# Two-block model on one core: the order of router, gather and tail in the experts, and of the matmuls in a feed-forward loop

## The chip, the core and the metric

One core of one Trainium2 chip runs the whole program in one launch. The metric is the device time of an execution in microseconds, as the median of several runs. The engines are named as in the profile: PE is TensorE (matmuls), PEld its loads of stationary operands, DVE VectorE, ACT ScalarE, POOL GpSimd, SP the engine whose queue issues most of the large loads. Everything is computed in float32; the large products split an operand into a high and a low part and add the products of the parts.

## The reference, cut to what matters

One sequence of 256 tokens with 1024 features passes through two blocks. The first block holds the experts that the change is about; the second is two layers, each with a feed-forward half, a mixing part and a second feed-forward half.

```python
# block 1
h = x
u = rmsnorm(h, norm_mix_g) @ w_in
o_sb = sb_group(u[..., :SB_IN], sb_out_g)          # stick-breaking attention
o_rw = rwkv7_group(u[..., SB_IN:], ...)            # a delta-rule recurrence
h = h + concatenate([o_sb, o_rw]) @ w_out
xn = rmsnorm(h, norm_ffn_g).reshape(256, 1024)
y = hier_moe(xn, ...)
h = rmsnorm(h + y, final_norm_g)

def hier_moe(x, w_grp, b_grp, w_exp, b_exp, w_gate, w_up, w_down):
    # 4 groups of 8 experts: the best group, then the best 2 of its 8
    grp_prob = softmax(x @ w_grp + b_grp);  g_val, g_idx = top_k(grp_prob, 1)
    sel = the 8 columns of (x @ w_exp + b_exp) that belong to g_idx
    e_val, e_idx = top_k(softmax(sel), 2)
    weights = g_val * e_val / sum(e_val)
    combine = for each token the weight of each of the 32 experts (30 are zero)
    for e in range(32):                            # w_gate, w_up: 1024x256, w_down: 256x1024
        y += combine[:, e:e+1] * ((silu(x @ w_gate[e]) * (x @ w_up[e])) @ w_down[e])

# block 2, the part that the change touches, four times
swiglu(x, w_gate, w_up, w_down) = (silu(x @ w_gate) * (x @ w_up)) @ w_down   # 1024 -> 2816 -> 1024
```

## The kernel before, in words

The 256 tokens are two blocks j = 0, 1 of 128, and the 1024 features are two halves n = 0, 1 of 512. `x` holds the residual stream, tokens on partitions.

**End of the projection (L936 to L954).** The output projection adds eight 128-row pieces f of `w_out` into four accumulators `acs[j, n]`. The pieces f = 4 to 7 come last, as the list `us`. Block 0 is finished first; for each half, `router.add` adds the residual and takes the squares, and `router.factor(0)` makes the factor of the norm. Then the half (1, 0) of the projection runs, then block 0's transposes (`turn`) and their copy out of PSUM (`turned`), then half (1, 1), and then the 16 small matmuls `logits` of block 0, eight for each half, with 36 columns (4 groups and 32 experts).

**Router (L983 to L1012, and L1273 to L1306).** Inside `Moe.run`, block 1 goes through the same steps. `select(j)` is a list of 12 small VectorE steps that picks group and experts; `ranks(j)` gives each token its slot in its expert, from two small matmuls with a triangular matrix, and `place` turns that into a one-hot matrix `OH[j]`. Each expert has 32 slots. `weave` issues the steps of two lists in turn. The three `with_x` matmuls that stand in between seed the accumulators `py[j, n]` with `x`; the fourth stands in round 0.

**Rounds (L1311 to L1347).** There are eight rounds q of four experts. `up` multiplies the gathered rows of four experts with gate (hf = 0) and up (hf = 1) matrices, 32 matmuls for each expert and round and half, the four experts on four strips of 32 rows. `act` makes silu(gate) * up * weight, transposes it and copies it to `hT`. `down` multiplies with the down matrices, for the two output halves one after the other. `back` splits a half into a high and a low part (`yh`, `yl`) and adds it into `py[j, n]` by a matmul with the transposed one-hot matrix, which brings the rows back to their tokens. The rows of the next round are gathered in the same round: `gather` multiplies `OH[j]` with `x` for j = 0, 1 and both halves into one PSUM tile `mx`, `gathered` copies half 0 by ScalarE and half 1 by VectorE into `xr`, and `rows_T` transposes `xr` and writes the gained rows `XG`.

**Weights (L1026 to L1052).** There are 96 loads of 1 MB: in each round four gate, four up and four down matrices. They go through the SP queue into 22 ring places, taken in the order of `order`. `load_next` issues the next ones as soon as the code has finished with older ones; a load waits until the place that it overwrites has been read. The places lie where the pools of the projection lie, so that the first 22 loads wait for the projection's tiles. One of those tiles is `kk0` (L436), which shares its memory with place `mw8`, the sixth in the order. The down matrix of expert 31, the last, is loaded in two halves of 512 output columns.

**Tail (L1350 to L1395).** After the last round the result stands in `py`. `gained` multiplies it with the final gain, `square` and `square_x` take the eight sums of squares that the final norm and the next norm need, and `back(7, y, 1)` stands behind the first `gained`.

**Order.** What is issued between `K.ordered = True` and `K.ordered = False` on PE, DVE and ACT keeps the order of the code (`keep_in_program_order`). Everything else, the loads on SP and POOL too, is put in order by the framework's planner from its estimates. The framework also orders accesses to one tile from the code, and adds the waits between engines.

**Feed-forward loop (L1728 to L1746).** A step i makes 256 of the 2816 hidden columns of gate and up, for both blocks; there are ten steps in each of four loops. Its weights come in four units of two 128-row pieces (`wh`, `wl`: the high and low part). For each unit, eight wide matmuls (512 columns: `wh` with both parts of X) and then eight narrow ones (256 columns: `wl` with the high part) are issued, over the four combinations of b (128 columns of the hidden ones) and s (gate or up).

Of the kernel before, what the change touches and what calls it, by code (L numbers as in the profile page):

```python
# [9 lines left out]
F32 = mybir.dt.float32  # L10
# [7 lines left out]
P = 128  # L18
# [287 lines left out]
class Front:  # L306
# [112 lines left out]
    def run(self, ctx, x, router):  # L419
# [523 lines left out]
        for n in range(2):  # L943
            if n:
                for h in range(2):
                    router.turn(x, 0, h)
                for h in range(2):
                    router.turned(0, h, xT[h])
            for f, u in us:
                out_mm(u, f, 1, n, False, f == 7)  # L950
        for n in range(2):
            router.logits(0, n, xT[n])
        K.ordered = False
        router.rest = [acs[1, n] for n in range(2)]  # L954
# [6 lines left out]
class Moe:  # L961
# [52 lines left out]
    def run(self, ctx, x, B=None):  # L1014
# [103 lines left out]
        def gather(q, j):  # L1118

            if j == 0:  # L1120
                pg[0] = K.mx.tile([P, 2, 512], F32, name="mx")
            for n in range(2):
                K.mm(pg[0][:, n], OH[j][:, 4 * q:4 * q + 4].rearrange("p e c -> p (e c)"), x[:, j, n * 512:(n + 1) * 512],
                     j == 0, j == 1, share=True)

        def gathered():
            xr[0] = wk.tile([P, 2, 512], F32, name="xr")
            V, S, _ = K.engines()
            S.activation(xr[0][:, 0], pg[0][:, 0], AF.Copy)
            V.tensor_copy(xr[0][:, 1], pg[0][:, 1])  # L1130

        def rows_T():

            pt = K.mx.tile([P, KD, P], F32, name="mx")
            r = xr[0].rearrange("p n f -> p (n f)")
            V, S, T_ = K.engines()
# [63 lines left out]
        def all_tokens(nmax):  # L1200
            v = nc.values_load(nmax[0:1, 0:1], min_val=0, max_val=2 * T)
            with tc.If(v > CAP):
# [7 lines left out]
                with tc.For_i(0, NE, 1) as e:  # L1210
# [13 lines left out]
                    for j in range(2):  # L1224
                        hT = self.act(wk, a[j], ce[:, j], self.r[j])
# [13 lines left out]
        def down(q, hT):  # L1239
            ys = []  # L1240
            for n in range(2):
                y = K.mx.tile([P, 512], F32, name="mx")
                for k in range(2):
                    for i in range(4):
                        K.mm(y[32 * i:32 * i + 32], hT[:, k, 32 * i:32 * i + 32],
                             W["d", 4 * q + i, 0][:, k, n * 512:(n + 1) * 512], k == 0, k == 1, share=True)
                ys.append(y)
            return ys
# [12 lines left out]
        def back(q, ys, n):  # L1261
            if q == 7 and n:
                t = spare("yr", 12, F32R)
                yh, yl = t[:, 0:512], t[:, 512:1024]
            else:
                yh, yl = [wk.tile([P, 512], F32R, name=t) for t in ("yh", "yl")]
            K.engines()[1].activation(yh, ys[n], AF.Copy)
            K.engines()[0].tensor_sub(yl, ys[n], yh)
            for y in (yh, yl):
                for j in range(2):  # L1270
                    K.mm(py[j, n], OHT[0][:, q % 2, j * P:(j + 1) * P], y, False, q == 7 and y is yl)

        K.ordered = True  # L1273
        xT = [wk.tile([P, 4, P], F32, name="xTm", tag=t) for t in ("XG1", "yh")]
# [3 lines left out]
        for n in range(2):  # L1278
            self.add(x, 1, n, self.rest[n], self.rest[n])
        for n in range(2):  # L1280
            self.turn(x, 1, n)
            self.turned(1, n, xT[n])
        for n in range(2):
            self.logits(1, n, xT[n])
        f1 = self.factor(1)
        run(f1[:4])
        weave(f1[4:], s0[:6])
        for n in range(2):
            with_x(0, n)
        weave(s0[6:], s1[:6])  # L1290
        K.mm(pr[:, 0], lt, mask[:, 0])
        K.mm(pr[:, 1], K.ones, mask[:, 0], stop=False, share=True)
        with_x(1, 0)
        run(s1[6:8])
        weave(s1[8:10], ranks(0))
        run(s1[10:])
        K.mm(pr[:, 1], lt, mask[:, 1], start=False, share=True)
        gather(0, 0)
# [7 lines left out]
        def rows(q):  # L1306
            for j in range(2):
                gather(q, j)
# [1044 lines left out]
```

## Time and profile before

| | |
|---|---|
| median of 3 runs | 1621.58 us (1621.26 to 1625.19) |
| profiled execution | 1625.12 us |
| its span | 1623.4 us |
| mean granted clock of PE | 0.981 of full speed |
| PE, DVE, ACT, POOL busy | 95%, 64%, 51%, 3% |
| DMA | 331.29 MB, mean 204 GB/s |

The span is the time from the first to the last instruction in the trace of one profiled execution; times in the rows further down count from its start. A row names the engine, the line of the code, the operation, the output and input tiles, and in brackets the idle time before it and what ended it. L48 stands for everything that is issued in the pinned order, since the helper on that line issues it. The experts lie between about 223 us, where the projection ends, and 447 us, where the final norm's first multiply starts; the four feed-forward loops begin at 464.48, 862.36, 1048.62 and 1446.89 us in the chain of waits.

### The profile page before, as it was taken

The numbers are of one execution on the slowest core, as the hardware profiler recorded it, in microseconds if no ns is written. First come the engines' busy times: TensorE is split into PE (matmuls) and PEld (weight loads), VectorE is DVE, ScalarE is ACT, GpSimd is POOL, SyncE is SP. The second block draws the span as 40 slices with busy tenths as digits, with TensorE's granted clock in tenths as the row PEclk, the third lists the DMA queues.
The fourth block names the chain that finished last, engine by engine and source line by source line (L and its number), as shares of the span: only waits on it lengthen the run. The fifth ranks groups of instructions, "written<-read, shape, count | busy, mean of one in ns | idle before, by whom it ended". The sixth has DMA issues, their size and how long they took to land.

```text
span 1623.4 us, 25106 instructions
## 1 busy us (share of the span) xinstructions
PE 1549.9 (95%) x9734; PEld 1283.6 (79%) x9734; DVE 1036.6 (64%) x1916; ACT 828.3 (51%) x1408; POOL 43.5 (3%) x134
## 2 busy tenths in 40 slices
PE   7999998887799999999999999999999999999998
PEld 6989874343378888889878888888888989778887
DVE  7866551111377656868986665666648779876653
ACT  6633421111356544668645554456546687455643
POOL 4000000000100000000000000000000000000000
PEclk9999998999999999999999999999999999999999
DMA  6431599999956555553456665656566434556653
GB/s 209 136 102 66 202 369 388 421 420 420 374 182 194 182 194 176 181 163 104 156 182 195 185 196 183 202 182 185 176 203 203 157 118 151 173 157 188 197 178 111
DMA packets 195644, 331.29 MB, mean 204 GB/s; under 512 B 11972, under 2 KB 150674, under 8 KB 183362
## 3 DMA queue, kind: packets, MB, share of 16 engines
q1 hardware_dynamic: 186208, 315.19, 56.4%
q0 software_dynamic: 4528, 13.41, 2.5%
q8 instruction: 77, 1.26, 0.3%
q10 hardware_dynamic: 4786, 1.05, 0.3%
q14 instruction: 45, 0.37, 0.1%
HBM read 328.25 MB, written 1.38 MB: 203 GB/s over the span
## 4 chain that ended last, share of the span: by engine, by line
PE 70%; DMA 6%; DVE 4%; ACT 2%; issue 1%; SPq 0%; ACTq 0%; DVEq 0%
PE acc L246 39%; PE mx L246 19%; PE acc L48 7%; PE mx L48 4%; DMA mw<-in_exp_w_down 2%; DMA mw<-in_exp_w_up 1%; DMA mw<-in_exp_w_gate 1%; DVE wl L258 1%; DVE wl L48 1%; PE mx L1969 0%; DMA wr<-in_w_in 0%; ACT wh L277 0%; PE mx L1993 0%; DMA wr<-in_ffn_w_up 0%; DVE ul L258 0%
## 5 line engine op out<-in xcount | busy, mean ns | idle before, releaser
L258 DVE TENSOR_TENSOR wl<-wr,wh 128x1024 fp32r<-128x1024 f32 x358 | 436.7, 1224 | 269.8 <-ACT wh L277 267.3
L277 ACT ACTIVATE wh<-wr 128x1024 fp32r<-128x1024 f32 x358 | 377.9, 1058 | 363.3 <-PE acc L246 249.5
L246 PE MATMUL acc<-X,wh 128*128 128x256 f32 (+1 forms) x1664 | 357.1, 329 | 0.0
L246 PEld LDWEIGHTS acc<-X,wh 128*128 128x128 f32 x1664 | 277.2, 191 | 25.4 <-issue 4.2
L246 PE MATMUL acc<-X,wl 128*128 128x256 f32 x1152 | 237.2, 284 | 0.0
L246 PEld LDWEIGHTS acc<-X,wl 128*128 128x128 f32 x1152 | 186.3, 191 | 6.9
L246 PE MATMUL mx<-X,wh 128*128 128x512 f32 x640 | 161.9, 393 | 0.0
L246 PEld LDWEIGHTS mx<-X,wh 128*128 128x128 f32 x640 | 114.5, 189 | 19.9
L246 PE MATMUL acc<-wh,hh 128*128 128x512 f32 x288 | 112.1, 389 | 0.0
L246 PE MATMUL acc<-wl,hh 128*128 128x512 f32 x288 | 112.1, 389 | 0.0
L246 PE MATMUL acc<-wh,hl 128*128 128x512 f32 x288 | 112.0, 389 | 0.0
L246 PEld LDWEIGHTS mx<-X,wl 128*128 128x128 f32 x640 | 88.3, 190 | 7.0
L246 PE MATMUL mx<-X,wl 128*128 128x256 f32 x640 | 90.5, 282 | 0.0
L48 PE MATMUL mx<-mw,XG 128*32 128x256 f32 x1024 | 64.6, 396 | 9.3 <-DMA mw<-in_exp_w_up 5.9
L48 PEld LDWEIGHTS mx<-mw,XG 128*32 128x32 f32 x1024 | 34.2, 114 | 37.9 <-issue 9.2
L246 PEld LDWEIGHTS acc<-wh,hl 128*128 128x128 f32 x288 | 54.1, 188 | 11.3
L246 PEld LDWEIGHTS acc<-wh,hh 128*128 128x128 f32 x288 | 54.1, 188 | 11.2
L246 PEld LDWEIGHTS acc<-wl,hh 128*128 128x128 f32 x288 | 54.1, 188 | 11.0
L246 PE MATMUL acc<-wh,m 128*128 128x512 f32 x192 | 61.4, 394 | 0.0
L48 DVE COPY xr<-mx 128x512 f32<-128x512 f32 x8 | 5.5, 691 | 74.1 <-ACT xr L48 74.1
L246 PE MATMUL acc<-xh,wh 128*128 128x256 f32 x176 | 50.3, 286 | 0.0
L246 PE MATMUL acc<-xh,wl 128*128 128x256 f32 x176 | 49.9, 283 | 0.0
(641 smaller groups left out, 2537.4 us busy)
## 6 DMA issues: line engine op xcount, KB each, us to landing
wr<-in_w_in SPq DMA_DIRECT2D x44, 1024.0 KB, 5.4
wr<-in_ffn_w_gate SPq DMA_DIRECT2D x88, 512.0 KB, 4.0
wr<-in_ffn_w_up SPq DMA_DIRECT2D x88, 512.0 KB, 5.1
wr<-in_ffn_w_down SPq DMA_DIRECT2D x40, 1024.0 KB, 5.0
mw<-in_exp_w_gate SPq DMA_DIRECT2D x32, 1024.0 KB, 14.8
mw<-in_exp_w_up SPq DMA_DIRECT2D x32, 1024.0 KB, 16.7
mw<-in_exp_w_down SPq DMA_DIRECT2D x31, 1024.0 KB, 17.6
wr<-in_w_out SPq DMA_DIRECT2D x20, 1024.0 KB, 5.0
```

Source lines behind the costliest of these rows:

```text
L48: return lambda *a, **k: self.tc.keep_in_program_order(f(*a, **k))
L246: self.engines()[2].matmul(out, l, r, start=start, stop=stop, skip_group_check=share)
L258: i = self.K.engines()[0].tensor_sub(l, v, h)
L277: self.K.engines()[1].activation(h, v[:, q:q + c], AF.Copy)
```

## The change

Five things change their place in the order; no large product is added or taken away.

- Router: block 0's transposes and logits move ahead, between the pieces of the projection's halves (1, 0) and (1, 1), and so do the add, the transposes, the copy and the logits of block 1's half 0. The new tile `xT1` holds that half; it borrows the place `kk0`. In `Moe.run` only half 1 of block 1 is left, and `select(0)` and `ranks(0)` run around it.
- Gather: `gather(q, j, n)` does one half at a time, and the copy of a half follows the second matmul of that half. In each round `act` yields behind the multiply (a generator now): the matmuls with block 0's rows stand between the multiply and the transposes of the activation, those with block 1's rows and the copies behind `hT`. `rows_T` stands behind the down matmuls of the second output half. The three `with_x` move into round 0, ahead of its down matmuls.
- Down and back: the first output half's copies (`out_rows`) are issued ahead of the second half's down matmuls. In round 7 the second half leaves out the fourth expert, whose two matmuls come in the tail, behind the first half's `back`.
- Tail: `gained` of half 0 comes first for both blocks, then the squares of (0, 0), then the rest of round 7's second half in pinned order, then the other squares, with `square_x(1, 0)` last.
- Feed-forward loop: for each (b, s) the two wide matmuls and then the two narrow ones, in place of eight wide and eight narrow ones in a row.

```diff
@@ -940,18 +940,27 @@
         run(router.factor(0))
-        for n in range(2):
-            if n:
-                for h in range(2):
-                    router.turn(x, 0, h)
-                for h in range(2):
-                    router.turned(0, h, xT[h])
-            for f, u in us:
+        def last(n, fu):
+            for f, u in fu:
                 out_mm(u, f, 1, n, False, f == 7)
-        for n in range(2):
-            router.logits(0, n, xT[n])
+        last(0, us[:2])
+        for h in range(2):
+            router.turn(x, 0, h)
+        for h in range(2):
+            router.turned(0, h, xT[h])
+        last(0, us[2:])
+        for h in range(2):
+            router.logits(0, h, xT[h])
+        last(1, us[:2])
+        router.rest = acs[1, 1]
+        router.add(x, 1, 0, acs[1, 0], acs[1, 0])
+        router.turn(x, 1, 0)
+        xT1 = ft([4, P], "xT1", "kk0")
+        router.turned(1, 0, xT1)
+        last(1, us[2:])
+        router.logits(1, 0, xT1)
         K.ordered = False
-        router.rest = [acs[1, n] for n in range(2)]
 NRING = 22
@@ -1115,25 +1124,25 @@
         XG, pg, xr = [None, None], [None], [None]
-        def gather(q, j):
-            if j == 0:
+        def gather(q, j, n):
+            if j + n == 0:
                 pg[0] = K.mx.tile([P, 2, 512], F32, name="mx")
-            for n in range(2):
-                K.mm(pg[0][:, n], OH[j][:, 4 * q:4 * q + 4].rearrange("p e c -> p (e c)"), x[:, j, n * 512:(n + 1) * 512],
-                     j == 0, j == 1, share=True)
-        def gathered():
-            xr[0] = wk.tile([P, 2, 512], F32, name="xr")
-            V, S, _ = K.engines()
-            S.activation(xr[0][:, 0], pg[0][:, 0], AF.Copy)
-            V.tensor_copy(xr[0][:, 1], pg[0][:, 1])
+            K.mm(pg[0][:, n], OH[j][:, 4 * q:4 * q + 4].rearrange("p e c -> p (e c)"), x[:, j, n * 512:(n + 1) * 512],
+                 j == 0, j == 1, share=True)
+            if j:
+                V, S, _ = K.engines()
+                if n:
+                    V.tensor_copy(xr[0][:, n], pg[0][:, n])
+                else:
+                    xr[0] = wk.tile([P, 2, 512], F32, name="xr")
+                    S.activation(xr[0][:, n], pg[0][:, n], AF.Copy)
         def rows_T():
             pt = K.mx.tile([P, KD, P], F32, name="mx")
+            V, S, T_ = K.engines()
             r = xr[0].rearrange("p n f -> p (n f)")
-            V, S, T_ = K.engines()
             for k in range(KD):
...
@@ -1236,16 +1245,11 @@
                          W["gu", 4 * q + i, hf][:, k], k + hf == 0, k == KD - 1, share=True)
-        def down(q, hT):
-            ys = []
-            for n in range(2):
-                y = K.mx.tile([P, 512], F32, name="mx")
-                for k in range(2):
-                    for i in range(4):
-                        K.mm(y[32 * i:32 * i + 32], hT[:, k, 32 * i:32 * i + 32],
-                             W["d", 4 * q + i, 0][:, k, n * 512:(n + 1) * 512], k == 0, k == 1, share=True)
-                ys.append(y)
-            return ys
+        def down_mm(q, hT, y, n, experts):
+            for k in range(2):
+                for i in experts:
+                    K.mm(y[n][32 * i:32 * i + 32], hT[:, k, 32 * i:32 * i + 32],
+                         W["d", 4 * q + i, 0][:, k, n * 512:(n + 1) * 512], k == 0, k == 1, share=True)
         def spare(name, slot, dt=F32):
@@ -1258,55 +1262,51 @@
             K.mm(py[j, n], K.ident, x[:, j, n * 512:(n + 1) * 512], True, False)
-        def back(q, ys, n):
+        yp = {}
+        def out_rows(q, y, n):
             if q == 7 and n:
                 t = spare("yr", 12, F32R)
-                yh, yl = t[:, 0:512], t[:, 512:1024]
+                yp[n] = t[:, 0:512], t[:, 512:1024]
             else:
-                yh, yl = [wk.tile([P, 512], F32R, name=t) for t in ("yh", "yl")]
-            K.engines()[1].activation(yh, ys[n], AF.Copy)
-            K.engines()[0].tensor_sub(yl, ys[n], yh)
-            for y in (yh, yl):
-                for j in range(2):
-                    K.mm(py[j, n], OHT[0][:, q % 2, j * P:(j + 1) * P], y, False, q == 7 and y is yl)
+                yp[n] = [wk.tile([P, 512], F32R, name=t) for t in ("yh", "yl")]
+            V, S, _ = K.engines()
+            S.activation(yp[n][0], y[n], AF.Copy)
+            V.tensor_sub(yp[n][1], y[n], yp[n][0])
+        def back(q, n):
+            yh, yl = yp[n]
+            for j, y in [(0, yh), (0, yl), (1, yh), (1, yl)] if q == 7 else [(0, yh), (1, yh), (0, yl), (1, yl)]:
+                K.mm(py[j, n], OHT[0][:, q % 2, j * P:(j + 1) * P], y, False, q == 7 and y is yl)
         K.ordered = True
-        xT = [wk.tile([P, 4, P], F32, name="xTm", tag=t) for t in ("XG1", "yh")]
+        xT = wk.tile([P, 4, P], F32, name="xTm", tag="XG1")
         OH[0] = K.xp.tile([P, NE, CAP], F32, name="OH0", tag="grow")
...
         s0, s1 = select(0), select(1)
-        for n in range(2):
-            self.add(x, 1, n, self.rest[n], self.rest[n])
-        for n in range(2):
-            self.turn(x, 1, n)
-            self.turned(1, n, xT[n])
-        for n in range(2):
-            self.logits(1, n, xT[n])
+        run(s0[:8])
+        self.add(x, 1, 1, self.rest, self.rest)
+        self.turn(x, 1, 1)
+        self.turned(1, 1, xT)
+        run(s0[8:])
         f1 = self.factor(1)
-        run(f1[:4])
-        weave(f1[4:], s0[:6])
-        for n in range(2):
-            with_x(0, n)
-        weave(s0[6:], s1[:6])
         K.mm(pr[:, 0], lt, mask[:, 0])
         K.mm(pr[:, 1], K.ones, mask[:, 0], stop=False, share=True)
-        with_x(1, 0)
-        run(s1[6:8])
-        weave(s1[8:10], ranks(0))
-        run(s1[10:])
+        run(f1[:3])
+        weave(f1[3:5], ranks(0))
+        run(f1[5:])
+        self.logits(1, 1, xT)
+        for n in range(2):
+            gather(0, 0, n)
+        run(s1)
         K.mm(pr[:, 1], lt, mask[:, 1], start=False, share=True)
-        gather(0, 0)
         run(ranks(1))
-        gather(0, 1)
-        gathered()
+        for n in range(2):
+            gather(0, 1, n)
         rows_T()
...
             place(j, 4, NE)
-        def rows(q):
-            for j in range(2):
-                gather(q, j)
-            gathered()
         for q in range(NE // 4):
@@ -1327,24 +1327,40 @@
                 slots_T(q)
-            if q != 7:
-                rows(q + 1)
             if q == 6 and B:
...
                 next(par)
-            hT = self.act(wk, a, ws[:, q:q + 1], ws[:, 8 + q:9 + q])
+            act = self.act(wk, a, ws[:, q:q + 1], ws[:, 8 + q:9 + q])
+            next(act)
+            if q != 7:
+                for n in range(2):
+                    gather(q + 1, 0, n)
+            hT = next(act)
+            if q != 7:
+                for n in range(2):
+                    gather(q + 1, 1, n)
+            if q == 0:
+                with_x(0, 0)
+                with_x(0, 1)
+                with_x(1, 0)
+            if q == 7 and B:
+                next(par, None)
+            y = [K.mx.tile([P, 512], F32, name="mx") for _ in range(2)]
+            down_mm(q, hT, y, 0, range(4))
+            out_rows(q, y, 0)
+            down_mm(q, hT, y, 1, range(3 if q == 7 else 4))
+            load_next(4)
             if q not in (1, 7):
                 rows_T()
-            if q == 7 and B:
-                next(par, None)
-            y = down(q, hT)
-            load_next(4)
+            back(q, 0)
             if q == 0:
...
                 with_x(1, 1)
-            for n in range(1 if q == 7 else 2):
-                back(q, y, n)
+            if q != 7:
+                out_rows(q, y, 1)
+                back(q, 1)
         K.ordered = False
@@ -1376,19 +1392,22 @@
             V.tensor_mul(x[:, j, half[n]], py[j, n], fg[:, half[n]])
-        gained(0, 0)
-        back(7, y, 1)
+        for j in range(2):
+            gained(j, 0)
+        square(0, 0)
+        square_x(0, 0)
+        K.ordered = True
+        down_mm(7, hT, y, 1, [3])
+        out_rows(7, y, 1)
+        back(7, 1)
+        K.ordered = False
         square(1, 0)
-        square(0, 0)
-        gained(1, 0)
-        gained(0, 1)
-        square_x(0, 0)
-        square(0, 1)
-        gained(1, 1)
-        square_x(0, 1)
-        square(1, 1)
+        for j in range(2):
+            gained(j, 1)
+        for j in range(2):
+            square(j, 1)
+            square_x(j, 1)
         square_x(1, 0)
-        square_x(1, 1)
         run(e0)
@@ -1400,10 +1419,11 @@
         V.scalar_tensor_tensor(sg, a[:, 256:512], w, sg, op0=OP.mult, op1=OP.mult)
+        yield
         for k in range(2):
...
         S.activation(hT, a[:, 512:768].rearrange("p (k t) -> p k t", k=2), AF.Copy)
-        return hT
+        yield hT
 NZ, NXBC, NDT = 0, 1024, 2560
@@ -1728,13 +1748,13 @@
             for wh, wl, k0, m in self.units(("gu", i), 0, KD):
-                bs = [(ac[b][s], slice(s * 256 + b * P, s * 256 + (b + 1) * P)) for b in range(2) for s in range(2)]
-                for a, c in bs:
-                    for k in range(m):
-                        K.mm(a, wh[:, k, c], X[:, k0 + k], k0 + k == 0, False, share=True)
-                for a, c in bs:
-                    for k in range(m):
-                        K.mm(a[:, 0], wl[:, k, c], X[:, k0 + k, 0], False, k0 + k == KD - 1, share=True)
+                for b in range(2):
+                    for s in range(2):
+                        a, c = ac[b][s], slice(s * 256 + b * P, s * 256 + (b + 1) * P)
+                        for k in range(m):
+                            K.mm(a, wh[:, k, c], X[:, k0 + k], k0 + k == 0, False, share=True)
+                        for k in range(m):
+                            K.mm(a[:, 0], wl[:, k, c], X[:, k0 + k, 0], False, k0 + k == KD - 1, share=True)
             if i == 1:
```

## Rows read from the trace of the kernel before

**Rows 1.** Chain of waits, 320 to 460 us: start us, length us, what.

```profile
373.25 20.90 DMA mw<-in_exp_w_up
```

**Rows 2.** Busy by stretch: PE, PEld, DVE, ACT, POOL (instructions); clock, DMA share, GB/s.

```profile
195.00:225.00 30.00, 30.00 (x168) 25.92 (x167) 17.50 (x47) 11.23 (x23) 0.00 (x0) 0.98 0.91 357
225.00:230.00 5.00, 4.75 (x32) 3.55 (x30) 3.80 (x28) 1.08 (x2) 0.00 (x0) 1.00 0.91 336
240.00:250.00 10.00, 9.31 (x119) 5.25 (x112) 2.39 (x15) 1.06 (x4) 0.00 (x0) 1.00 0.90 343
270.00:280.00 10.00, 10.00 (x135) 5.22 (x135) 0.07 (x1) 0.00 (x0) 0.00 (x0) 0.93 0.86 335
280.00:385.00 105.00, 89.31 (x849) 41.89 (x851) 15.80 (x25) 19.57 (x47) 0.00 (x0) 0.98 1.01 421
```

**Rows 3.** Timeline, SP queue: start us, length us, line, what, number in the group.

```profile
194.51 1.28 SPq L1046 DMA_DIRECT2D mw<-in_exp_w_up  x3
...
226.81 17.08 SPq L1051 DMA_DIRECT2D mw<-in_exp_w_down  x4
...
261.46 14.64 SPq L1051 DMA_DIRECT2D mw<-in_exp_w_down  x4
```

**Rows 4.** Timeline of TensorE, 222 to 240 us: the router.

```profile
222.98 1.87 PE L48 MATMUL acc<-wrt,xT 128*128 128x36 f32 x16
...
226.01 1.98 PE L48 MATMUL acc<-wrt,xTm 128*128 128x36 f32 x16 [0.25 <-ACT xTm L48]
227.81 1.96 PE L48 MATMUL acc<-x,ident 128*128 128x512 f32 x4
...
231.35 3.68 PE L48 MATMUL mx<-x,OH 128*128 128x512 f32 x8
```

**Rows 5.** Timeline, VectorE and ScalarE, first gather; then the page's group.

```profile
231.77 0.29 DVE L48 TENSOR_TENSOR OH<-sl,rank 128x128 f32<-128x128 f32 x1
235.06 0.60 ACT L48 ACTIVATE xr<-mx 128x512 f32<-128x512 f32 x1 [8.62 <-PE mx L48]
235.69 0.69 DVE L48 COPY xr<-mx 128x512 f32<-128x512 f32 x1 [3.63 <-ACT xr L48]
...
L48 DVE COPY xr<-mx 128x512 f32<-128x512 f32 x8 | 5.5, 691 | 74.1 <-ACT xr L48 74.1
```

**Rows 6.** Timeline of TensorE, 238 to 272 us: round 0, round 1's first matmuls.

```profile
238.38 7.11 PE L48 MATMUL mx<-mw,XG 128*32 128x256 f32 x128 [0.79 <-DVE XG L48]
...
253.97 0.54 PE L48 MATMUL mx<-ident,msg 128*128 128x128 f32 x2 [3.06 <-DVE msg L48]
...
271.28 1.09 PE L48 MATMUL mx<-mw,XG 128*32 128x256 f32 x16
```

**Rows 7.** Timeline of POOL's queue, 380 to 404 us.

```profile
386.78 0.55 POOL L1322 DMA_DIRECT2D fg<-in_final_norm_g  x1 [209.27 <-DMA mw<-in_exp_w_up]
403.09 0.56 POOL L115 DMA_DIRECT2D par<-in_ssd_conv_w  x1 [15.76 <-PE mx L48]
```

**Rows 8.** Timeline, 434 to 449 us: the tail, in order of start.

```profile
435.29 1.04 PE L48 MATMUL mx<-mw,mhT 128*32 128x512 f32 x2 [1.47 <-DMA mw<-in_exp_w_down]
...
440.20 0.72 PE L48 MATMUL acc<-yh,OHT 128*128 128x512 f32 x2
...
441.43 0.60 ACT L48 ACTIVATE fsq<-acc 128x512 f32<-128x512 f32 x1 [0.52 <-PE acc L48]
...
447.06 1.42 DVE L48 SCALAR_TENSOR_TENSOR xn<-x,nri,grow 128x512 f32<-128x512 f32 x2 [0.45 <-ACT fsq L48]
```

**Rows 9.** Feed-forward: two steps of the chain, then TensorE's timeline from 864 us.

```profile
487.41 11.17 PE acc L246 x64
...
576.80 48.99 PE acc L246 x216
...
864.51 0.28 PE L246 MATMUL acc<-X,wl 128*128 128x256 f32 x1
...
865.55 0.63 PE L246 MATMUL acc<-X,wl 128*128 128x256 f32 x4
```

More of the change, by code (lines that the diff above doesn't have):

```diff
@@ L1224, in all_tokens @@
                     for j in range(2):
-                        hT = self.act(wk, a[j], ce[:, j], self.r[j])
+                        _, hT = self.act(wk, a[j], ce[:, j], self.r[j])
                         for n in range(2):
```

## Prediction

> **What bounds the kernel now.** The span is 1623.4 us and TensorE is busy for 95% of it, so the first view to read is the chain of waits, to see where the end is set by something else. Nearly all of it is matmuls, except in the experts, where it runs through loads of expert weights, as in the 20.90 us from 373.25 on [rows 1]. The stretches say why: from 280 to 385 us the DMA engines are busy at a share of 1.01 and move 421 GB/s, although TensorE still works for 89 of those 105 us [rows 2]. A load is 1.05 MB, so it costs 1.05 / 0.421 = 2.49 us, and the 96 of them leave back to back. From about 280 us on, a faster TensorE buys nothing; only a load stream that ends sooner, or a shorter tail behind the last load, moves the end of this stage. Everything after it (four feed-forward halves, two mixing parts) is TensorE-bound again.
>
> Before 280 us the stream has holes. Against a share of 1.01, the stretch 225 to 230 lacks 0.10 x 5 = 0.5 us, 240 to 250 lacks 0.11 x 10 = 1.1 us, and 270 to 280 lacks 0.15 x 10 = 1.5 us [rows 2]. The queue's rows say what they wait for: a ring place that TensorE has not finished reading. The group issued from 226.81 us takes 17.08 us because its third load waits for the first half of round 0's up matmuls, and the one from 261.46 us takes 14.64 us because it waits for that half of round 1 [rows 3]. So these edits can give the stage 3.1 us at most, 0.2% of the time.
>
> **The change, part by part.**
>
> Router. Before, 16 small logits matmuls of token block 0 (1.87 us) come behind the last projection matmul, at 222.98 us; then the half norms, transposes and 16 logits matmuls of block 1 (1.98), three identity matmuls that seed the output (1.96 for two, so 2.9), and the gather of 3.68 [rows 4]. The change puts block 0's logits, half of block 1's transposes (0.5 us) and one more half of logits inside the projection. The last projection matmul comes 1.87 + 0.5 = 2.4 us later, at 225.4. From there: before, add, square, transposes and the first copy took from 222.98 to the second logits at 226.01, 3.0 us; I take 0.7 off, an estimate: block 0's logits held TensorE until 224.85, while one add (0.7, as the copy in rows 5) and its issue are over about 1.1 us after 222.98. I add 1.0 for the last eight logits matmuls; together 3.3. Block 0's gather half (1.85) then runs beside VectorE's selection of block 1, which woven with block 0's took from the logits' end at 226.01 + 1.98 = 227.99 to 231.77 + 0.29 = 232.06 [rows 4, 5], 4.1 us; alone I give it 3.6. Then the second gather half, 0.9 per output half.
>
> Here lies the point that decides the copies. Before, the ACT copy of the first half starts at 235.06 and the DVE copy of the other half at 235.69, not together: the page's group of the eight xr copies on VectorE has 74.1 us of idle time ahead of them, and all 74.1 are ended by the ACT copy, though the two read different halves of the PSUM tile [rows 5]. The framework orders all accesses of one such tile. The new code writes half 0, copies it, then writes half 1; by the same ordering the second matmul waits for the copy. So I count 0.9 + 0.7 + 0.9 + 0.7 = 3.2 rather than an overlap; then transposes 1.2 and the gain 0.7. The sum is 3.3 + 3.6 + 3.2 + 1.9 = 12.0, so round 0 starts at 237.5 in place of 238.38 [rows 6]: 0.9 us earlier.
>
> The Trainium skill (PSUM — Partial Sum Buffer, "Summary: rules for kernel authors") advises to read one bank while a matmul writes another, and the two halves are two banks. By that rule the copy would be hidden and the router 0.7 us shorter; the 74.1 us say otherwise for this program.
>
> Round 0. Its up matmuls take 7.1 us. Before, TensorE then idles 3.06 us ahead of the transposes of the activation, behind the gather, the copies and ACT's table load [rows 6]. In the change the Silu goes ahead of the copies, and half of the gather covers it: about 2.4 us saved. The second gather half waits for a copy, 0.7 us. The three seeding matmuls, 2.9 us, now stand here, ahead of the down matmuls. The transposes of the gathered rows move behind them. So the down matmuls end about 1 us earlier, and with less idle time behind them I place round 1's up matmuls at 269.3 in place of 271.28: 2 us earlier. The first ring places come free 0.9 us earlier, the ones that the second hole waits for 2 us earlier: the 240 to 250 hole gives back 0.8, the 270 to 280 hole all of its 1.5.
>
> One thing speaks against this. The new tile that holds block 1's first transposed half borrows the place kk0 of the projection's pool, and by the pool's sizes kk0 lies in ring place 8, which the sixth load takes. Before, that load leaves at 194.51 [rows 3]. Now it must wait for block 1's first logits, at about 226.4. The queue is filled in the order of a planner, which lets a ready load pass a blocked one: on POOL the fg load, from round 7 of the code, leaves at 386.78, and the par loads of round 6 at 403.09 [rows 7]. So I expect the other loads to pass it; it is then one load more (2.5 us) behind that time, but block 0's transposed tiles, on which the seventeenth load waits, come free 2.5 us earlier and close the 0.5 us hole, and the queue has room in the two later holes. I charge 0.5 net. Stage: -0.8 - 1.5 + 0.5 = -1.8. Bounds: -3.1 with all holes closed; +1.7 if the load leaves last of the first 22, so that round 0's up matmuls of that expert wait about 5 us.
>
> Rounds 1 to 6. The gain ahead of the down matmuls (some 1.9 us) is given back behind them, since the transposes of the gathered rows now stand between the two output halves. About +0.5 us each, an estimate. The load stream hides it: TensorE waits for loads in round 6 [rows 1]. If that cover were gone it would cost 3 us over six rounds.
>
> Tail. The last expert's second half is taken out of the down matmuls and put behind the first output half's scatter. Its two passes alone take 1.04 us [rows 8], and its four run one after the other on one strip of the array: about 1.9 us. Before, they lay beside the other experts' and were done when the first half's scatter began, at 440.20 [rows 8]. Now that scatter goes first (from 439.4, when its copy is made, to about 440.7), and the half is done at 442.6 on the old scale, 2.4 us later. ACT fills that with squares, which before started at 441.43 and now at 440.5. Copy (0.6), difference (0.7) and scatter (0.5) of the late half end at 444.4, and five of the eight squares are then left. Before, eight ran from 441.43 to 447.06, 0.70 each [rows 8], so five end at 447.9. The norm's first multiply waits for the last of them (its 0.45 us idle is ended by ACT's square) and comes at 447.9 in place of 447.06. So +0.8; bounds -0.9 (squares start that much earlier and nothing else is late) and +2.4 (nothing hides the late half).
>
> Feed-forward loops. Four loops of ten steps; a step is 64 matmuls in 11.17 us [rows 9], 16 groups of two wide ones (512 columns) and two narrow ones (256), so a group costs 11.17 / 16 = 698 ns, though the two kinds run eight and eight. The change issues them two and two, in the same number. Nothing waits newly: the chain runs from step to step on TensorE alone, so the narrow operands are there in time. A short run stands in the trace at another place, where one narrow and four wide ones alternate with longer runs: 865.55 - 864.51 = 1.04 us [rows 9]. With 2w + 2n = 698 and 4w + n = 1040 a wide one is 230 ns and a narrow one 119. Two equations for two unknowns assume that the order costs nothing; what bears it out is that 230 lies close to the 48.99 / 216 = 227 ns of the down matmuls [rows 9], which are all wide. So I take 0. Bounds: at 227 ns a wide one, with the narrow one unchanged, a group takes 2 x 3 = 6 ns less, and 4 x 160 groups 4 us less; if the narrow one of the short run took half of 227, its wide ones took 232, a group 3 ns more, the loops +2 us.
>
> Sum: -1.8 + 0.8 + 0 = -1.0 us. The profiled execution took 1625.12 us with a span of 1623.4, so 1.7 lie around the span; the median of the three runs shown is 1621.58, 3.5 below it. The difference is carried over: 1621.6 - 1.0 = 1620.6 us.
>
> **Rivals.**
>
> The blocked load holds the queue. If the queue keeps the code's order, the sixth load and all behind it wait from 194.5 to 226.4. Before, the stretch 195 to 225 moved 357 GB/s [rows 2], so 30 x 0.357 / 1.05 = 10 loads, at 2.49 us each 25 us of stream, and the stream sets the end: 1621.6 + 25 = 1646. It decides as soon as one load waits that others can't pass. For it: the queue takes one instruction at a time, and its group from 261.46 takes 14.64 us because of such a wait [rows 3]. Against it: rows 7. 10%.
>
> All upper ends: the load leaves late (+1.7), the late half is not hidden (+2.4), the short runs restart slowly (+2): 1621.6 + 6.1 = 1627.7. For it: each of these places has a wait in the rows. Against: they are independent. 12%.
>
> All lower ends: -3.1 - 0.9 - 4 = -8: 1613.6. For it: the holes are there, and the wide matmuls do run at 227 ns elsewhere. Against: the ordered PSUM accesses, and the start of every run of wide ones. 18%.
>
> **How the numbers follow.** A measurement of this kernel can tell about 0.3%, 4.9 us. The forecast, with its neighbours within that bound, has 60%, its own range 1617 to 1625; faster 18%; slower 10 + 12 = 22%. The range of 1613 to 1628 leaves out the first rival and the outer ends of the other two.
>
> **What would show it.** Right: in the profile after, the share of DMA at 270 to 280 us is near 1; the last expert load lands 1 to 3 us earlier; one load of an up matrix leaves near 226 us and others leave ahead of it; the second gather matmul waits for an ACT copy; the multiply xn waits for a square and comes 0 to 1 us after the old distance from the last landing; a feed-forward step still takes 11.17 us. Wrong: a hole in the load stream between 195 and 225 us (the first rival), feed-forward steps that differ by over 1%, or a stage after the experts that changes by more than 2 us.

## The result, and the profile after

The changed kernel took 1648.95 us (median; 1644.96 to 1651.93) against 1623.38 us: a ratio of 1.0146, 95% interval 1.0125 to 1.0168. It is slower by 1.5%, outside the range of 1613 to 1628, and near the 1646 of the first rival, which had 10%. The profiled execution took 1651.93 us, the longest of the four; its span is 1650.3.

The busy time by stretch of the changed kernel, to be read beside [rows 2]:

```profile
195.00:225.00 30.00, 30.00 (x169) 26.05 (x168) 19.09 (x53) 11.56 (x23) 0.00 (x0) 0.97 0.00 1
225.00:230.00 5.00, 4.95 (x33) 4.01 (x32) 3.16 (x18) 1.91 (x4) 0.00 (x0) 1.00 0.30 88
...
240.00:250.00 10.00, 9.22 (x133) 4.59 (x131) 4.37 (x14) 1.61 (x7) 0.00 (x0) 0.77 1.01 423
...
270.00:280.00 10.00, 9.72 (x107) 5.08 (x110) 0.93 (x3) 0.00 (x0) 0.00 (x0) 0.74 1.01 420
```

For 30 us, from 195 to 225, the DMA engines move next to nothing (1 GB/s, before 357). From 230 us on they are busy without a hole (a hole is a stretch with a DMA share below 1.01). The holes of [rows 2] are gone, most likely because the stream is so late that the places have been read by then.

The SP queue of the same kernel (as [rows 3]: start, length, what, number of issues):

```profile
175.98 5.67 SPq L1055 DMA_DIRECT2D mw<-in_exp_w_gate  x3
181.71 46.92 SPq L1055 DMA_DIRECT2D mw<-in_exp_w_up  x4
228.68 2.25 SPq L1060 DMA_DIRECT2D mw<-in_exp_w_down  x4
```

The four up loads of round 0 take 46.92 us to issue: the first leaves at 181.71, the second (the sixth load, into the place of kk0) at 227.35, just after block 1's first logits (226.24 + 0.97). Everything behind it leaves afterwards.

TensorE in the router, as [rows 4] and [rows 6], and then the feed-forward chain, as [rows 9]:

```profile
226.24 0.97 PE L48 MATMUL acc<-wrt,xT 128*128 128x36 f32 x8
...
229.44 1.96 PE L48 MATMUL mx<-x,OH 128*128 128x512 f32 x4
232.64 0.41 PE L48 MATMUL acc<-mask,lt 128*128 128x32 f32 x2 [1.24 <-DVE mask L48]
233.65 1.51 PE L48 MATMUL mx<-x,OH 128*128 128x512 f32 x2 [0.61 <-DVE OH L48]
235.85 2.07 PE L48 MATMUL mx<-x,OH 128*128 128x512 f32 x2 [0.69 <-ACT xr L48]
238.71 1.97 PE L48 MATMUL mx<-ident,xr 128*128 128x128 f32 x8 [0.79 <-DVE xr L48]
241.46 8.59 PE L48 MATMUL mx<-mw,XG 128*32 128x256 f32 x128 [0.78 <-DVE XG L48]
...
254.08 0.51 PE L48 MATMUL mx<-ident,msg 128*128 128x128 f32 x2 [0.33 <-DVE msg L48]
```

```profile
503.16 11.28 PE mx L246 x64
514.44 11.15 PE acc L246 x64
525.59 11.15 PE mx L246 x64
```

The second gather half waits for the ACT copy, as forecast. But the same matmuls take longer than before: the 128 up matmuls 8.59 us (7.11 in [rows 6]), and the eight transposes ahead of them 1.97 (forecast 1.2). A feed-forward step takes 11.15 us in place of 11.17, the second step of a loop 11.28 in place of 11.18; from the first step's start to the down matmuls the four loops are 0.28 + 0.12 + 0.14 + 0.12 = 0.66 us shorter together.

The tail, as [rows 8]; the last expert weights land at 462.45 us:

```profile
463.12 0.60 ACT L48 ACTIVATE yh<-mx 128x512 fp32r<-128x512 f32 x1 [4.31 <-PE mx L48]
...
465.41 1.90 PE L48 MATMUL mx<-mw,mhT 128*32 128x512 f32 x4
465.77 0.60 ACT L48 ACTIVATE fsq<-acc 128x512 f32<-128x512 f32 x1 [2.05 <-DVE x L48]
...
468.73 0.97 PE L48 MATMUL acc<-yr,OHT 128*128 128x512 f32 x3 [0.23 <-DVE yr L48]
469.26 1.29 DVE L48 TENSOR_TENSOR x<-acc,fg 128x512 f32<-128x512 f32 x2 [0.59 <-PE acc L48]
469.99 0.60 ACT L48 ACTIVATE fsq<-acc 128x512 f32<-128x512 f32 x1 [1.46 <-DVE x L48]
...
473.55 1.41 DVE L48 SCALAR_TENSOR_TENSOR xn<-x,nri,grow 128x512 f32<-128x512 f32 x2 [0.59 <-ACT fsq L48]
```

The norm's first multiply xn comes 473.55 - 462.45 = 11.10 us after the last landing; before, 447.06 - 437.98 = 9.08.

The part ahead of the experts differs by up to 7.3 us between the profiles below, so they are compared from a common point: the start of the last of the four matmuls that transpose the mixing output (`mx<-ident,go`), which the change does not touch. Round 0 and round 1 are the starts of their up matmuls. Each row is one profiled execution, in us:

| kernel | point | round 0 | round 1 | last landing | landing to xn | xn to end |
|---|---|---|---|---|---|---|
| before | 215.15 | 23.24 | 56.13 | 222.83 | 9.08 | 1176.36 |
| after | 216.10 | 25.36 | 58.03 | 246.35 | 11.10 | 1176.70 |
| e1_other_place | 216.62 | 24.99 | 58.17 | 225.41 | 11.10 | 1175.13 |
| e2_before_kk0 | 210.96 | 23.26 | 56.22 | 244.80 | 9.11 | 1175.75 |
| e3_load_late | 216.01 | 25.92 | 58.99 | 224.94 | 18.75 | 1176.10 |
| e4_load_mid | 212.79 | 24.96 | 58.14 | 232.38 | 18.76 | 1173.17 |
| f1_seeds_in_router | 218.02 | 23.22 | 52.24 | 221.39 | 11.07 | 1174.77 |
| f2_old_tail | 212.61 | 24.98 | 58.32 | 225.84 | 8.99 | 1176.03 |
| f3_seeds_and_tail | 218.27 | 23.19 | 52.16 | 220.91 | 9.01 | 1177.06 |
| f4_before_no_seeds | 215.45 | 26.03 | 60.63 | 227.19 | 9.09 | 1173.72 |

Rounds and last landing count from the point, the point itself from the start of the span. The kernels e1 to f4 are those of the experiments below. The span of the changed kernel grew by 1650.3 - 1623.4 = 26.9 us: 23.52 up to the last landing, 2.02 in the tail, 0.95 ahead of the point and 0.34 behind xn.

### The profile page after: what moved, and what is told of

Read it like the earlier page. It is cut to its first block, busy times and chain, and to the rows that moved or that the text cites. A ratio compares the mean times of both kernels' runs of the same rounds, so it can differ in the third digit from the quotient of the medians.

```text
span 1650.3 us, 24962 instructions
## 1 busy us (share of the span) xinstructions
PE 1568.9 (95%) x9734; PEld 1287.2 (78%) x9734; DVE 1040.4 (63%) x1916; ACT 836.7 (51%) x1408; POOL 43.6 (3%) x134
## 4 chain that ended last, share of the span: by engine, by line
PE 80%; DMA 11%; DVE 4%; ACT 3%; issue 1%; ACTq 0%; POOL 0%; SPq 0%; DVEq 0%
PE acc L246 46%; PE mx L246 20%; PE acc L48 9%; DMA mw<-in_exp_w_up 4%; DMA mw<-in_exp_w_down 4%; PE mx L48 4%; DMA mw<-in_exp_w_gate 2%; DVE wl L258 1%; DVE wl L48 1%; DMA cr<-csd 0%; ACT wh L277 0%; PE mx L1989 0%; DMA wr<-in_w_in 0%; PE mx L2013 0%; DMA sub<-d 0%
## 5 line engine op out<-in xcount | busy, mean ns | idle before, releaser
L246 PE MATMUL acc<-X,wh 128*128 128x256 f32 (+1 forms) x1664 | 397.0, 330 | 0.0
L246 PE MATMUL acc<-X,wl 128*128 128x256 f32 x1152 | 273.0, 282 | 0.0
L246 PEld LDWEIGHTS acc<-X,wh 128*128 128x128 f32 x1664 | 260.7, 191 | 5.3 <-issue 4.2
L246 PEld LDWEIGHTS acc<-X,wl 128*128 128x128 f32 x1152 | 218.7, 190 | 28.6
L246 PE MATMUL mx<-X,wh 128*128 128x512 f32 x640 | 201.6, 396 | 0.0
L246 PEld LDWEIGHTS mx<-X,wl 128*128 128x128 f32 x640 | 120.2, 188 | 28.4
L246 PE MATMUL mx<-X,wl 128*128 128x256 f32 x640 | 125.8, 278 | 0.0
L48 PE MATMUL mx<-mw,XG 128*32 128x256 f32 x1024 | 82.6, 461 | 20.6 <-DMA mw<-in_exp_w_up 17.8
L246 PEld LDWEIGHTS mx<-X,wh 128*128 128x128 f32 x640 | 97.5, 189 | 0.2
L48 PEld LDWEIGHTS mx<-mw,XG 128*32 128x32 f32 x1024 | 40.4, 131 | 62.2 <-issue 24.9
L246 PEld LDWEIGHTS acc<-wh,hl 128*128 128x128 f32 x288 | 54.1, 188 | 11.2
L246 PEld LDWEIGHTS acc<-wl,hh 128*128 128x128 f32 x288 | 54.1, 188 | 11.2
```

Of the source, the lines that this page charges most:

```text
L48: return lambda *a, **k: self.tc.keep_in_program_order(f(*a, **k))
L246: self.engines()[2].matmul(out, l, r, start=start, stop=stop, skip_group_check=share)
```

## Experiments

### e1: the tile in another place

```diff
-        xT1 = ft([4, P], "xT1", "kk0")
+        xT1 = ft([4, P], "xT1", "Vk0")
```

> The changed kernel, with one word different: the tile xT1 borrows Vk0, which the block 0 logits have read by then, in place of kk0. Vk0 lies in the place of the seventeenth load. Theory A (the sixth load is blocked and every load behind it stands in the queue): the sixth load leaves near 195 us again, the last load lands at 438 to 440 us in place of 462.45, and the time is 1622 to 1627 us: what stays over the kernel before is the longer tail. Theory B (the new order of the router work and of the copies costs the time itself: round 0 starts at 241.46 in place of 238.38, and TensorE falls to a clock of 0.71 there): the time stays above 1640 us.

Measured: 1630.25 us, ratio to before 1.0035 (1.0021 to 1.0048); the kernel before took 1625.44 us in the runs beside e1 to e4. The queue again, and the busy time by stretch (columns as [rows 2]):

```profile
182.15 15.05 SPq L1055 DMA_DIRECT2D mw<-in_exp_w_up  x4
...
227.81 1.76 SPq L1055 DMA_DIRECT2D mw<-in_exp_w_up  x4
229.68 18.42 SPq L1060 DMA_DIRECT2D mw<-in_exp_w_down  x4
```

```profile
225.00:240.00 15.00, 11.63 (x51) 7.12 (x50) 7.24 (x35) 2.51 (x5) 0.00 (x0) 0.85 0.88 345
240.00:250.00 10.00, 9.21 (x124) 4.78 (x126) 4.37 (x14) 1.60 (x7) 0.00 (x0) 0.71 0.75 297
...
270.00:280.00 10.00, 9.72 (x94) 5.28 (x98) 0.93 (x3) 0.00 (x0) 0.00 (x0) 0.68 0.88 365
```

The sixth load leaves at 195.93 and the last landing comes 246.35 - 225.41 = 20.9 us earlier. Theory A holds for these 20.9 us. By the ratios e1 gives back 1.46 - 0.35 = 1.1%, some 18 us; the two intervals leave about 4 us either way. But 1630 is above the 1622 to 1627 of A: round 0 is still 1.75 us later than before, the landing 2.6. The holes in the load stream are back and larger: counted as in the prediction, 0.13 x 15 + 0.26 x 10 + 0.13 x 10 = 5.9 us, before 3.1. A part of this is the new place's own: the seventeenth load now waits for `xT1` and leaves at 227.81, 11.2 us after the point; before, it left 9.8 us after it.

### e2: the kernel before, with that one place

```diff
-        xT = [ft([4, P], "xT", f"Vk{h}") for h in range(2)]
+        xT = [ft([4, P], "xT", t) for t in ("Vk0", "kk0")]
```

> The kernel before, with one word different: of block 0's two transposed tiles the second borrows kk0 in place of Vk1. Nothing of the changed order is in it. Theory A: the sixth load leaves at about 225 us, after block 0's last logits matmul (224.85), and all others behind it. In the changed kernel it left at 227.35 and the last landing came 24.5 us later; 2.4 us less gives 22, so 1645 us. Theory B: one load of 2.5 us comes late, at most 1625 us.

Measured: 1647.67 us, 1.0141 (1.0125 to 1.0157), 22 us by the medians (1625.44 before). The queue of this kernel:

```profile
176.57 45.54 SPq L1046 DMA_DIRECT2D mw<-in_exp_w_up  x4
```

One borrowed place gives the old order nearly the whole loss; its last landing is 21.97 us later. From the leaving of the sixth load (220.83) to the last landing it is 455.76 - 220.83 = 234.93 us here, and 462.45 - 227.35 = 235.10 in the changed kernel. The two kernels differ in router, rounds and tail, and it makes 0.2 us: as long as this load is blocked, the queue sets the last landing.

### e3 and e4: the same load later in the order

Both stand on the changed kernel, with the tile in `kk0`; one edit or the other is made.

```diff
-        order = [*range(3, 15), 0, 1, 15, 16, 2, *range(17, NRING)]
+        order = [*range(3, 8), *range(9, 15), 0, 1, 15, 16, 2, 8, *range(17, NRING)]   # e3
+        order = [*range(3, 8), *range(9, 14), 8, 14, 0, 1, 15, 16, 2, *range(17, NRING)]   # e4
```

> The changed kernel, with xT1 in kk0, but the ring place that kk0 lies in is the seventeenth in the order of loads and not the sixth. Theory A: sixteen loads leave before the blocked one, as in the kernel before; the last load lands at 438 to 440 us, 1621 to 1627 us. A theory by which the shared memory itself is dear, wherever its load stands (or theory B): 1640 us or more.

> The same, with that place the eleventh in the order. Theory A gives a dose: ten loads and not five land before the queue stops, the rest starts at 227.4 as in the changed kernel, so 5 x 2.49 = 12.5 us of the 24.5 come back: 1636 us, the last landing at 450. Theory B: as the changed kernel, 1649. If the planner let loads pass: as the kernel before.

Measured: e3 1636.75 us, 1.0061 (1.0044 to 1.0078); e4 1640.53, 1.0103 (1.0084 to 1.0122). By the landings both bear out A: the same tile in the same memory costs 23.5 us with its load sixth in the queue, 9.6 with it eleventh and 2.1 with it seventeenth (246.35, 232.38, 224.94 against 222.83). Moving it five loads back gave 14.0 us, where five loads make 12.5.

The times missed (1621 to 1627 and 1636 were expected), in the main by a side effect of the edit: the new order puts the last load of all into place 11, which the final gain fg borrows. In e3, POOL's queue and VectorE:

```profile
447.21 0.53 POOL L1322 DMA_DIRECT2D fg<-in_final_norm_g  x1 [17.70 <-PE mx L48]
...
451.15 1.29 DVE L48 TENSOR_TENSOR x<-acc,fg 128x512 f32<-128x512 f32 x2 [7.12 <-DMA fg<-in_final_norm_g]
```

VectorE waits 7.12 us for fg, and the tail is 18.75 us, 7.65 more than in e1; in e4 it is 18.76.

### f1 to f4: what was left in e1

Busy time by stretch, 236 to 244 us, of the kernel before and then of the changed one (columns as [rows 2]; the clock is the number ahead of the DMA share):

```profile
236.00:240.00 4.00, 2.77 (x40) 1.98 (x44) 2.75 (x4) 1.14 (x4) 0.00 (x0) 1.00 1.02 430
240.00:244.00 4.00, 4.00 (x80) 2.39 (x76) 2.01 (x12) 0.47 (x3) 0.00 (x0) 1.00 0.90 334
```

```profile
232.00:236.00 4.00, 2.07 (x5) 0.75 (x5) 1.18 (x6) 0.60 (x1) 0.00 (x0) 0.78 1.00 418
236.00:240.00 4.00, 3.21 (x8) 1.64 (x9) 0.69 (x1) 0.00 (x0) 0.00 (x0) 0.50 1.01 426
240.00:244.00 4.00, 3.22 (x28) 1.46 (x30) 3.14 (x7) 1.61 (x7) 0.00 (x0) 0.50 1.01 428
```

The granted clock fell to 0.50, the 1.2 GHz level, after a stretch in which TensorE was busy for 2.07 of 4 us. In the kernel before, the seeding matmuls stand in the waits of the selection, and the clock is at 1.00 from 228 to 252 us.

f1, f2 and f3 all have the tile in `Vk0`, as e1 has it. The edit of f1 and f3 to the seeds:

```diff
+        with_x(0, 0)                   # f1, f3: behind block 0's gather
         run(s1)
...
-        for n in range(2):
-            gather(0, 1, n)
+        gather(0, 1, 0)
+        with_x(0, 1)
+        gather(0, 1, 1)
+        with_x(1, 0)
...
-                with_x(0, 0)           # no longer in round 0
-                with_x(0, 1)
-                with_x(1, 0)
```

f2 and f3 take the tail of the kernel before (four experts in round 7's second half, gains and squares in the old order); f3 has both edits. f4 does the opposite of f1 on the kernel before: the three seeds go from the router to round 0, ahead of its down matmuls.

> The changed kernel with xT1 in Vk0 (e1_other_place), and the three seeding matmuls with_x out of round 0 and back between the router's gathers, where TensorE waits. In e1 TensorE waits there, its granted clock from 236 to 244 us is 0.50 (before: 1.00), and round 0 starts 24.99 us after the last transposes of the mixing output, mx<-ident,go (before: 23.24). Clock theory: without the idle places the clock stays at 1.00, round 0 starts at about 22.6, its up matmuls take 7.1 us and not 9.11, and the last load lands at 221 to 222.5 us after the same point (e1: 225.41): the time is 3 to 4 us under that of e1. Rival (the ordered copies and the longer selection set the router's length, not the clock): round 0 at 24.5 or later, and the three seeds only stand in the way: the time as e1 or above.

> e1_other_place with the tail of the kernel before: the last expert's second half is multiplied with the others, gains and squares in the old order. If the new tail costs what the trace says, the norm's multiply comes 9.1 us after the last landing and not 11.10, and the time is 2.0 us under that of e1. If the new tail hides something that the old order would show, less than 1 us.

> Both edits. The gains add up: 5 to 6 us under e1_other_place (which stood 0.35% over the kernel before), so 1 us under the kernel before to level with it. If they don't add up (the load stream hides the earlier rounds), 2 us under e1.

> The kernel before, with the three seeds taken out of the router and put ahead of round 0's down matmuls, nothing else. Clock theory: the waits in the selection grow, the clock falls to 0.50 around 232 to 240 us, and round 0's up matmuls take 8.5 us or more in place of 7.11; round 0 starts at 23.2 us after mx<-ident,go or later although 2.9 us of matmuls are gone, and the time is 1 to 4 us over the kernel before. Rival: the seeds only cost their time; round 0 starts up to 0.9 us earlier, its up matmuls take 7.1 us, time as before or less.

Measured against the kernel before in the same runs (1623.21 us): f1 1624.71, ratio 1.0004 (0.9992 to 1.0017); f2 1626.05, 1.0013 (0.9998 to 1.0027); f3 1620.09, 0.9978 (0.9964 to 0.9991); f4 1627.16, 1.0020 (1.0006 to 1.0035). A stretch of f1 and TensorE's timeline there; then the same two views of f4:

```profile
236.00:240.00 4.00, 4.00 (x14) 1.77 (x13) 0.69 (x1) 0.60 (x1) 0.00 (x0) 1.00 1.01 418
```

```profile
237.39 1.12 PE L48 MATMUL mx<-x,OH 128*128 128x512 f32 x2
...
239.29 1.16 PE L48 MATMUL mx<-ident,xr 128*128 128x128 f32 x8
241.23 7.11 PE L48 MATMUL mx<-mw,XG 128*32 128x256 f32 x128 [0.78 <-DVE XG L48]
```

```profile
228.00:232.00 4.00, 1.51 (x10) 1.29 (x9) 3.10 (x19) 0.00 (x0) 0.00 (x0) 0.78 0.94 383
232.00:236.00 4.00, 4.00 (x6) 1.70 (x6) 0.48 (x2) 0.00 (x0) 0.00 (x0) 0.50 1.01 426
236.00:240.00 4.00, 2.58 (x8) 0.99 (x7) 0.69 (x1) 0.60 (x1) 0.00 (x0) 0.87 1.01 426
```

```profile
231.87 6.25 PE L48 MATMUL mx<-x,OH 128*128 128x512 f32 x8
...
241.48 7.11 PE L48 MATMUL mx<-mw,XG 128*32 128x256 f32 x128 [0.78 <-DVE XG L48]
```

- f1: the clock stays at 1.00 up to 262 us, transposes take 1.16 and the up matmuls 7.11 again; round 0 starts 1.77 us earlier than in e1 (forecast 2.4), round 1 5.9, and the last landing 4.0. More matmuls in the router made it shorter: the 1.77 us are the last gather half (1.12 for 2.07) and the transposes (1.16 for 1.97). The 5.9 and the 4.0 are not the clock's alone, since round 0 is also rid of the seeds, 2.74 us in the changed kernel.
- f4: the other way round. The eight gather matmuls take 6.25 us where [rows 4] has 3.68, round 0 starts 2.8 us later and the last landing 4.4. The up matmuls, forecast at 8.5 or more, took 7.11: the clock was back by 240 us. Of the 2.8 us, 2.6 sit in the gather.
- f2: landing to xn 8.99 for 11.10, 2.1 us less, about what the trace gave (2.0). By their intervals neither f1 nor f2 can be told from the kernel before.
- f3: the gains add up. It is 0.22% under the kernel before (0.09 to 0.36%), with the landing 1.9 us earlier and the tail as before. Against e1 that is 0.57%, 9 us where 5 to 6 were expected; landing and tail of the two profiles give 4.5 + 2.1 = 6.6. The two ratios come from different runs and leave about 3 us either way.

## Why the prediction was wrong

**The step that failed** is in the paragraph on kk0: the queue "lets a ready load pass a blocked one ... So I expect the other loads to pass it", charged with 0.5 us. It was 20.9 by the last landings of the changed kernel and e1. Nothing passed: in every profile the expert loads leave in the code's order, and e3 and e4 moved the loss only by moving the load in that order. The evidence was wrong in kind. Rows 7 show that on POOL a later piece of code was placed ahead of an earlier one when the program was built; they don't show a queue that steps over a waiting load when it runs. [rows 3], which I put down for the rival, showed that: one wait holds its group for 14.64 us.

**The rival's size.** It counted 10 loads x 2.49 = 25 us. The measured loss has two parts: the last landing, 23.5 us later, and the tail, 2.0. The landing is the blocked queue's, as the 235 us of e2 show; the 2.6 us of a later stage don't add to it and only show once the load is moved (e1). The rival left out that the holes of 3.1 us close when the stream is late, and it had no tail. The two errors work against each other, so that 1646 came so close to 1649 is in part luck.

**Router: wrong by 2.7 to 3.0 us.** Round 0 was to start 0.9 us earlier (the step's own terms, 225.4 + 12.0, make 237.4 and not 237.5, 1.0 earlier); it starts 1.75 (e1) to 2.1 us (after) later. The logits end 13.51 us after the point, 0.7 later than the 12.83 of before, as forecast. The selection took 233.65 - 229.61 = 4.0 us for 3.6. The rest are durations that were forecast at full clock and ran, wholly or in part, at half: gather halves 1.51 and 2.07 for 0.9 each, transposes 1.97 for 1.2. I moved the seeds as if only their own time went with them; they also kept TensorE busy. The Trainium skill (TensorE: Matmul & The Clock Gate, "Why this matters for your kernels") asks to keep TensorE busy and warns of long idle gaps between bursts of matmuls. f1 and f4 agree with the first (granted clock 1.00 with the seeds in the waits, 0.50 without). On the gaps the measurement decides: the clock fell although no gap in TensorE's row was longer than 1.24 us, or 1.31 in f4.

**Stage: wrong also without the blocked load.** It was to end 1.8 us earlier; with the load unblocked it ends 2.6 us later (e1), and the holes grow in place of closing: round 0 starts late, its up matmuls run slowly, and the seventeenth load waits for the new place. How the 2.6 us divide between these was not measured. With the seeds in the gaps (f1, f3) the last load lands 1.4 and 1.9 us earlier than before. That this is close to 1.8 is luck: the forecast had the seeds in round 0, and these two kernels don't.

**Copies: right.** The second gather half waits for the ACT copy (0.69 us idle). Whether two PSUM tiles would avoid it was not tried.

**Round 0: terms right, start wrong.** TensorE's idle time ahead of the activation's transposes fell from 3.06 to 0.33 us, 2.7 less (forecast 2.4), the second gather half waits 0.75 us for its copy (0.7), and the seeds take 2.74 (2.9). Its up matmuls, put at 7.1 us, took 8.59, the first part of them at a clock of 0.50.

**Rounds 1 and 2: sign wrong, no effect.** They were to be 0.5 us longer each. From one round's first up matmul to the next's, e1 takes 21.6 us for the 24.3 of before, then 23.6 for 24.1. The cause was not looked at; the sum counts nothing for these rounds, because the loads hide them.

**Tail: sign right, size +2.0 for +0.8, inside its bounds.** The late half ended 469.70 - 462.45 = 7.25 us after the landing, where the step had 444.4 - 437.98 = 6.4: 0.8 of the missing 1.2 us. The five squares behind it were to start when its scatter ends. They were issued behind the gain multiplies of the same half, ACT idles 1.46 us until `DVE x`, and the first of them starts 0.3 us after the scatter's end.

**Feed-forward: right.** 0 forecast, -0.7 us measured. The upper bound of +2 us doesn't follow from its own numbers: with a wide one of 232 ns and a narrow one of 113.5 (half of 227) a group takes 2 x 232 + 2 x 113.5 = 691 ns, less than 698.

## What to carry to other kernels

Before a tile is given a borrowed place, look up which queued transfer overwrites that place and what stands behind it in the queue: the price is the whole queue for as long as the tile is read, not one transfer. Evidence on the order in which a program was built is no evidence that a queue reorders when it runs. A matmul that stands in a wait can be worth more than its time: before moving it, see what the clock does to the work behind the gap.

## What was not expected of the hardware

The granted clock went to 0.50 in a stretch whose longest single gap in TensorE's row was 1.24 us, and stayed there from 236 to 244 us of the changed kernel although TensorE was busy for 3.2 of every 4 us. In f4, where the longest gap ahead of the fall was 1.31 us, it recovered by 240 us, after a stretch from 232 to 236 in which TensorE was busy throughout.
